# Rotary embedding on one core: the first store is issued right after its own row, and three one-element copies that held two stores are taken out

## The chip, the cores and the metric

The kernel runs on 1 core of a Trainium2 chip. A core has several engines that run side by side, each with its own instruction queue: VectorE (DVE in the profile), ScalarE (ACT), GpSimd (POOL), TensorE (PE, not used here) and SyncE (SP). They meet through semaphores. Data move between the memory of the chip (HBM) and the core's SBUF (128 partitions) by DMA: an engine issues a transfer, and 16 DMA engines carry it out.

The metric is the device time of one execution in microseconds (us), as the median of several runs. Before: 316.28 us, median of 3 runs (316.09 to 316.48). Less is better.

## The reference

`x` has 8 batches x 2048 positions x 16 heads x 64 numbers, all float32. Neighbouring pairs of the 64 are rotated by an angle that depends on the position:

```python
x_pairs = x.reshape(batch, seq_len, num_heads, head_dim // 2, 2)
x1 = x_pairs[..., 0]
x2 = x_pairs[..., 1]
out1 = x1 * cos - x2 * sin
out2 = x1 * sin + x2 * cos
out = np.stack([out1, out2], axis=-1).reshape(batch, seq_len, num_heads, head_dim)
```

`cos` and `sin` have 2048 x 32 numbers. Input and output are 67.1 MB each, and the arithmetic is three operations per number.

## The kernel before

**Tiling.** One batch is called a row here. The 2048 positions of a row are laid over 128 partitions, 16 positions (K) to each, so that a row is a tile of 128 partitions x 16,384 numbers. Rows are kept in bf16 in `xt`, a buffer with five places; `HOME` says which row has which place: rows 0 to 4 have a place each, and rows 5, 6 and 7 take over those of rows 0, 1 and 2. In HBM a row is float32, 8.39 MB; in SBUF it is bf16, half of that, and the conversion is done by the DMA itself.

**Work on a row.** `rotate(b)` makes three VectorE operations: L89 writes `qt` = row x sine table, L92 multiplies the row in its place by the cosine table, L97 adds `qt`, with the two of each pair swapped, to the row. `qt` is one buffer (the pool has one slot), so that each rotation reuses it. Row 0 is rotated in two pieces, 4 positions and 12.

**Order.** The order is written out by hand (`manual_schedule`); each engine works through its instructions in program order, and the semaphore waits follow from the tiles that an instruction reads and writes.

- SP loads the first 4 positions of row 0 as float32 (L101), ACT converts them (L108).
- POOL issues, one behind the other and all on one DMA queue (q0 in the profile): the rest of row 0 (L102), the cosines and sines (L103, L104), `load(1, 2)` for rows 1 and 2 in one transfer, `load(3, 2)` for rows 3 and 4 (L70 is the line inside `load`).
- VectorE makes the tables (L110 to L112) and rotates row 0.
- `rotate(1)`, then `rotate(2)` with `between=first_store`: after L89 of row 2, `first_store` puts two copies of one element on ACT. L120 copies the last element of `qt` into `gate`, so ACT waits for L89 of row 2. L121 copies an element of row 0 onto itself, so that it counts as a writer of row 0; `store(0, 1)` (L74 inside `store`), which reads row 0, waits for it.
- L126 copies one element of the last place of `xt` (row 4) into `mark` on POOL, so POOL waits there until `load(3, 2)` has landed. Then come, on POOL, `store(1, 2)` (waits for row 2's rotation), `load(5, 1)` (takes row 0's place, so it waits until `store(0, 1)` has landed) and `load(6, 2)` (waits for `store(1, 2)`).
- `rotate(3)`, `rotate(4)`, `store(3, 2)`, `rotate(5)`, `rotate(6)`, `store(5, 2)`, `rotate(7)`. The last row is converted to float32 by ACT in four pieces (L138) into places 3 and 4 of `xt` (`wide`) and stored by SP (L139) on a queue of its own (q1).

Of the kernel before, what the change touches and what calls it, by code (L numbers as in the profile page):

```python
# [2 lines left out]

# [4 lines left out]


@with_exitstack  # L10
def kernel(
    ctx: ExitStack,
    tc: tile.TileContext,
    x: bass.AP,
    cos: bass.AP,
    sin: bass.AP,
    out: bass.AP,
):
    nc = tc.nc
    fp32 = mybir.dt.float32  # L20
    bf16 = mybir.dt.bfloat16
    mult = mybir.AluOpType.mult
    add = mybir.AluOpType.add

    B, S, H, D = x.shape
    P = 128
    K = S // P
    KP = 16
    D2 = D // 2
    HD = H * D  # L30
    NX = 5
    HEAD = 4
    PART = 4
    STAGE = 3


    HOME = [0, 1, 2, 3, 4, 0, 1, 2]

    x_t = x.rearrange("b (p k) h d -> b p k (h d)", p=P, k=K)
    out_t = out.rearrange("b (p k) h d -> b p k (h d)", p=P, k=K)  # L40
    x_r = x.rearrange("b (p k) h d -> p b (k h d)", p=P, k=K)
    out_r = out.rearrange("b (p k) h d -> p b (k h d)", p=P, k=K)
    cos_t = cos.rearrange("(p k) c -> p (k c)", p=P, k=K)
    sin_t = sin.rearrange("(p k) c -> p (k c)", p=P, k=K)

    consts = ctx.enter_context(tc.tile_pool(name="consts", bufs=1))
    stage = ctx.enter_context(tc.tile_pool(name="stage", bufs=1))

    xt = consts.tile([P, NX, K * HD], bf16)
    cos_sb = consts.tile([P, K * D2], fp32)  # L50
    sin_sb = consts.tile([P, K * D2], fp32)
    c_tab = consts.tile([P, K, D], bf16)
    s_tab = consts.tile([P, K, D], bf16)

    wide = (
        xt[:, STAGE : STAGE + 2]
        .rearrange("p a c -> p (a c)")
        .bitcast(fp32)
        .rearrange("p (k c) -> p k c", c=HD)
    )  # L60

    gate = consts.tile([1, 1], bf16)
    mark = consts.tile([1, 1], bf16)

    def home(b, k0=0, k1=K):
        return xt[:, HOME[b], k0 * HD : k1 * HD].rearrange("p (k c) -> p k c", c=HD)

    def load(b, n):
        h = HOME[b]
        nc.gpsimd.dma_start(out=xt[:, h : h + n], in_=x_r[:, b : b + n])  # L70

    def store(b, n):
        h = HOME[b]
        nc.gpsimd.dma_start(out=out_r[:, b : b + n], in_=xt[:, h : h + n])  # L74

    def rotate(b, k0=0, k1=K, between=None):
        nk = k1 - k0
        xp = home(b, k0, k1)
        qt = stage.tile([P, KP, HD], bf16, name="qt", tag="work")

        def rows(a):
            return a.rearrange("p k (h e) -> p k h e", h=H, e=D)

        def tab(a):
            return dataclasses.replace(
                a, offset=a.offset + k0 * D, ap=[a.ap[0], [D, nk], [0, H], [1, D]]
            )

        nc.vector.tensor_tensor(out=rows(qt[:, :nk]), in0=rows(xp), in1=tab(s_tab), op=mult)  # L89
        if between is not None:  # L90
            between(qt)
        nc.vector.tensor_tensor(out=rows(xp), in0=rows(xp), in1=tab(c_tab), op=mult)  # L92
        q_swap = dataclasses.replace(
            qt, offset=qt.offset + 1, ap=[qt.ap[0], [2, nk * HD // 2], [-1, 2]]
        )
        x3 = xp.rearrange("p k (a j) -> p (k a) j", j=2)
        nc.vector.tensor_tensor(out=x3, in0=x3, in1=q_swap, op=add)  # L97

    with tc.manual_schedule():
        head = stage.tile([P, HEAD, HD], fp32, name="st", tag="work")  # L100
        nc.sync.dma_start(out=head[:, :HEAD], in_=x_t[0, :, :HEAD])  # L101
        nc.gpsimd.dma_start(out=home(0, HEAD), in_=x_t[0, :, HEAD:])  # L102
        nc.gpsimd.dma_start(out=cos_sb, in_=cos_t)  # L103
        nc.gpsimd.dma_start(out=sin_sb, in_=sin_t)  # L104
        load(1, 2)
        load(3, 2)

        nc.scalar.copy(out=home(0, 0, HEAD), in_=head[:, :HEAD])  # L108
        s2 = s_tab.rearrange("p k (i j) -> p (k i) j", j=2)
        nc.vector.tensor_copy(out=s2[:, :, 0], in_=sin_sb)  # L110
        nc.vector.tensor_scalar_mul(s2[:, :, 1], sin_sb, -1.0)  # L111
        nc.vector.tensor_copy(  # L112
            out=c_tab.rearrange("p k (i j) -> p (k i) j", j=2),
            in_=cos_sb.to_broadcast([P, K * D2, 2]),
        )
        rotate(0, 0, HEAD)
        rotate(0, HEAD, K)

        def first_store(qt):
            nc.scalar.copy(out=gate, in_=qt[:1, KP - 1, HD - 1 :])  # L120
            nc.scalar.copy(out=xt[:1, HOME[0], :1], in_=xt[:1, HOME[0], :1])  # L121
            store(0, 1)

        rotate(1)
        rotate(2, between=first_store)
        nc.gpsimd.tensor_copy(out=mark, in_=xt[:1, 4, K * HD - 1 :])  # L126
        store(1, 2)
        load(5, 1)
        load(6, 2)
        rotate(3)  # L130
        rotate(4)
        store(3, 2)
        for b in range(5, B):
            rotate(b)
            if b == 6:
                store(5, 2)
        for k in range(0, K, PART):
            nc.scalar.copy(out=wide[:, k : k + PART], in_=home(B - 1, k, k + PART))  # L138
        nc.sync.dma_start(out=out_t[B - 1], in_=wide)  # L139


# [1 line left out]
_INS = ['x', 'cos', 'sin']  # L143
_OUTS = [((8, 2048, 16, 64), 'float32')]


# [23 lines left out]
```

## Time and profile before

The profiled execution has a span of 314.3 us from the first to the last instruction; what lies around the span is in the run's time and not in the profile.

| what | value |
|---|---|
| median of 3 runs | 316.28 us |
| lowest and highest | 316.09, 316.48 us |
| span of the profiled execution | 314.3 us |
| granted clock | 1.000 |
| L89, L92, L97 each, on a whole row | 8.69 us, 7 times |
| VectorE waits for loads (L89) | 34.3 us in 3 waits, the longest 12.4 us |
| POOL waits: for L121 / for L97 / for stores to land (L70) | 93.4 / 91.5 / 43.1 us |
| last row's conversion on ACT (L138) | 4 x 3.60 us, from 269.31 |
| last store, issue to landing | 30.0 us, issued at 283.46 |

The transfers on q0 in the order of issue, with the time of issue and the time from there to landing (us):

| transfer | issued | to landing |
|---|---|---|
| rest of row 0 | 1.25 | 21.1 |
| rows 1 and 2 in | 3.0 | 59.3 |
| rows 3 and 4 in | 3.7 | 97.3 |
| row 0 out (first store) | 97.91 | 22.5 |
| rows 1 and 2 out (second store) | 115.04 | 44.1 |
| row 5 in | 120.67 | 57.6 |
| rows 6 and 7 in | 159.44 | 57.4 |
| rows 3 and 4 out | 167.52 | 88.0 |
| rows 5 and 6 out | 243.40 | 55.6 |

How to read it: "busy" is the time in which an engine executes; an instruction that waits for a semaphore is idle time in front of it, and the profile names what ended it ("releaser"). In lines of the timeline, the first number is the start in us from the span's start, the second the duration in us, and the bracket the idle time before and its releaser. A POOL line of the kind DMA_DIRECT2D is the issue of a transfer, not the transfer. The row "DMA" of the page gives the busy share of the 16 DMA engines in 40 slices of the span in tenths (9 is 90% or more); in a stretch, a share near 1 means that all 16 had work throughout, and it can come out a little over 1, since packets are long against the stretch and a packet on its border is counted on one side. The GB/s count the SBUF side of a transfer, which for loads is half the size of the HBM side.

### The profile page before, as it was taken

How to read it: one execution, taken by the hardware profiler on the slowest of the kernel's cores; microseconds unless marked ns; L12 is line 12 of the kernel's file. 1: busy time of each engine (PE TensorE's matmuls, PEld its weight loads, DVE VectorE, ACT ScalarE, POOL GpSimd, SP SyncE). 2: the span in 40 equal slices, each digit the busy share in tenths (PEclk: the TensorE clock that was granted, in tenths of full speed). 3: DMA queues.
4: the chain of work that ended last, by engine and by line, in shares of the span. 5: the costliest groups of instructions: out<-in, count | busy, mean ns of one | idle time of the engine just before them, and what ended most of it. 6: DMA issues, size and time to landing. Idle time of an engine off the chain costs nothing.

```text
span 314.3 us, 114 instructions
## 1 busy us (share of the span) xinstructions
DVE 210.3 (67%) x30; ACT 19.3 (6%) x8; POOL 12.4 (4%) x16
## 2 busy tenths in 40 slices
DVE  0009995099999999999992299903999999200000
ACT  1030000000000000000000000000000000790000
POOL 4000000000002400000000000000000000000000
DMA  7999999999999999999999999999999999999996
GB/s 253 264 284 200 200 200 267 200 200 204 263 200 267 409 525 400 400 425 509 400 200 225 242 200 200 234 234 334 400 509 425 400 400 525 409 400 400 525 409 267
DMA packets 2512, 102.24 MB, mean 325 GB/s; under 512 B 208, under 2 KB 208, under 8 KB 336
## 3 DMA queue, kind: packets, MB, share of 16 engines
q0 software_dynamic: 2224, 91.75, 92.1%
q1 hardware_dynamic: 288, 10.49, 8.0%
HBM read 67.63 MB, written 67.11 MB: 429 GB/s over the span
## 4 chain that ended last, share of the span: by engine, by line
DVE 67%; another core or an unknown queue 11%; ACT 3%; ACTq 1%; issue 0%; DVEq 0%
DVE xt L92 22%; DVE xt L97 22%; DVE qt L89 22%; ACT xt L138 3%; ACTq L165 1%; DVE c_tab L112 0%; DVEq L89 0%; DVEq L92 0%
## 5 line engine op out<-in xcount | busy, mean ns | idle before, releaser
L89 DVE TENSOR_TENSOR qt<-xt,s_tab 128x16384 bf16<-128x16384 bf16 (+2 forms) x9 | 69.7, 7743 | 34.5 <-DMA xt<-in_x_dram 34.3
L92 DVE TENSOR_TENSOR xt<-xt,c_tab 128x16384 bf16<-128x16384 bf16 (+2 forms) x9 | 69.7, 7743 | 0.4
L97 DVE TENSOR_TENSOR xt<-xt,qt 128x16384 bf16<-128x16384 bf16 (+2 forms) x9 | 69.7, 7743 | 0.3
L138 ACT CAST xt<-xt 128x4096 f32<-128x4096 bf16 x4 | 14.1, 3601 | 171.7 <-DVE xt L97 171.7
L110 DVE CAST s_tab<-sin_sb 128x512 bf16<-128x512 f32 x1 | 0.5, 454 | 23.8 <-DMA sin_sb<-in_sin_dram 23.8
L74 POOL DMA_DIRECT2D out_dram<-xt x4 | 2.7, 670 | 184.9 <-ACT xt L121 93.4
L126 POOL COPY mark<-xt 1x1 bf16<-1x1 bf16 x1 | 5.0, 5019 | 2.6 <-DMA xt<-in_x_dram 2.6
L120 ACT COPY gate<-qt 1x1 bf16<-1x1 bf16 x1 | 0.2, 192 | 78.6 <-DVE qt L89 78.6
L70 POOL DMA_DIRECT2D xt<-in_x_dram x4 | 2.7, 696 | 43.1 <-DMA out_dram<-xt 43.1
L108 ACT CAST xt<-st 128x4096 bf16<-128x4096 f32 x1 | 3.6, 3605 | 13.1 <-DMA st<-in_x_dram 13.1
L108 ACT ACT_TABLE_LOAD x1 | 1.3, 1283 | 0.7 <-PEq L154 0.7
L102 POOL DMA_DIRECT2D xt<-in_x_dram x1 | 0.7, 680 | 0.8 <-PEq L165 0.8
L112 DVE CAST c_tab<-cos_sb 128x1024 bf16<-128x1024 f32 x1 | 0.7, 685 | 0.0
L103 POOL DMA_DIRECT2D cos_sb<-in_cos_dram x1 | 0.6, 569 | 0.0
L104 POOL DMA_DIRECT2D sin_sb<-in_sin_dram x1 | 0.6, 562 | 0.0
L111 DVE TENSOR_SCALAR s_tab<-sin_sb 128x512 bf16<-128x512 f32 x1 | 0.4, 444 | 0.0
L121 ACT COPY xt<-xt 1x1 bf16<-1x1 bf16 x1 | 0.2, 188 | 0.0
L154 POOL MEMSET const-float32-0.0<- 128x1 f32 x1 | 0.1, 99 | 0.2 <-issue 0.2
L154 POOL MEMSET const-bfloat16-1.0<- 128x1 bf16 x1 | 0.1, 102 | 0.0
L154 POOL MEMSET const-float32-1.0<- 128x1 f32 x1 | 0.1, 99 | 0.0
L154 POOL MEMSET const-uint8-127<- 128x1 uint8 x1 | 0.1, 99 | 0.0
## 6 DMA issues: line engine op xcount, KB each, us to landing
xt<-in_x_dram POOLq DMA_DIRECT2D x3, 8192.0 KB, 59.3
xt<-in_x_dram POOLq DMA_DIRECT2D x1, 4096.0 KB, 57.6
xt<-in_x_dram POOLq DMA_DIRECT2D x1, 3072.0 KB, 21.1
st<-in_x_dram SPq DMA_DIRECT2D x1, 2048.0 KB, 14.4
cos_sb<-in_cos_dram POOLq DMA_DIRECT2D x1, 256.0 KB, 21.2
sin_sb<-in_sin_dram POOLq DMA_DIRECT2D x1, 256.0 KB, 21.3
out_dram<-xt POOLq DMA_DIRECT2D x4, 49.9
out_dram<-xt SPq DMA_DIRECT2D x1, 30.0
```

The lines of the kernel that those rows point to most:

```text
L70: nc.gpsimd.dma_start(out=xt[:, h : h + n], in_=x_r[:, b : b + n])
L74: nc.gpsimd.dma_start(out=out_r[:, b : b + n], in_=xt[:, h : h + n])
L89: nc.vector.tensor_tensor(out=rows(qt[:, :nk]), in0=rows(xp), in1=tab(s_tab), op=mult)
L92: nc.vector.tensor_tensor(out=rows(xp), in0=rows(xp), in1=tab(c_tab), op=mult)
L97: nc.vector.tensor_tensor(out=x3, in0=x3, in1=q_swap, op=add)
L102: nc.gpsimd.dma_start(out=home(0, HEAD), in_=x_t[0, :, HEAD:])
L103: nc.gpsimd.dma_start(out=cos_sb, in_=cos_t)
L108: nc.scalar.copy(out=home(0, 0, HEAD), in_=head[:, :HEAD])
L112: nc.vector.tensor_copy(out=c_tab.rearrange("p k (i j) -> p (k i) j", j=2), in_=cos_sb.to_broadcast([P, K * D2, 2]),)
L126: nc.gpsimd.tensor_copy(out=mark, in_=xt[:1, 4, K * HD - 1 :])
L138: nc.scalar.copy(out=wide[:, k : k + PART], in_=home(B - 1, k, k + PART))
L165: with _tile.TileContext(nc) as tc:
```

## The change

`store(0, 1)` moves up in the program to stand right behind the rotation of row 0, where it waits for that rotation alone. The copies L120, L121 and L126 go, with the tiles `gate` and `mark`, and `rotate` loses the parameter that let `first_store` run in its middle. `store(1, 2)` stays where it was; ahead of it on POOL there is now only the first store. All transfers keep their sizes and their order on POOL.

```diff
-    gate = consts.tile([1, 1], bf16)
-    mark = consts.tile([1, 1], bf16)
-
...
-    def rotate(b, k0=0, k1=K, between=None):
+    def rotate(b, k0=0, k1=K):
...
-        if between is not None:
-            between(qt)
...
         rotate(0, 0, HEAD)
         rotate(0, HEAD, K)
 
-        def first_store(qt):
-            nc.scalar.copy(out=gate, in_=qt[:1, KP - 1, HD - 1 :])
-            nc.scalar.copy(out=xt[:1, HOME[0], :1], in_=xt[:1, HOME[0], :1])
-            store(0, 1)
-
+        store(0, 1)
         rotate(1)
-        rotate(2, between=first_store)
-        nc.gpsimd.tensor_copy(out=mark, in_=xt[:1, 4, K * HD - 1 :])
+        rotate(2)
         store(1, 2)
         load(5, 1)
         load(6, 2)
```

## The prediction

> **What bounds the kernel now.** I read the page first: the span, the share of each engine, the DMA rows.
>
> ```profile
> span 314.3 us, 114 instructions
> DVE 210.3 (67%) x30; ACT 19.3 (6%) x8; POOL 12.4 (4%) x16
> ...
> DMA  7999999999999999999999999999999999999996
> ...
> q0 software_dynamic: 2224, 91.75, 92.1%
> q1 hardware_dynamic: 288, 10.49, 8.0%
> HBM read 67.63 MB, written 67.11 MB: 429 GB/s over the span
> ```
>
> No compute engine is near full (DVE 67%), but the DMA row is at 9 in all slices but the first and the last: the kernel is a stream of 134.7 MB at 429 GB/s. The chain of waits puts 67% on DVE and 11% on "another core or an unknown queue"; it follows DVE because the last store hangs on the last rotation, but the three pieces of 10.57, 11.05 and 12.33 us without an owner are DVE waiting for loads. So I ask when the 16 DMA engines lack work, and cut the span at the landings (issue time plus the time from issue to landing of that transfer). Columns: stretch, its length, DVE, ACT and POOL busy, clock, DMA share, GB/s.
>
> ```profile
> 62.00:101.00 39.00, 38.44 (x5) 0.29 (x2) 0.55 (x1) 1.00 1.00 229
> 101.00:120.60 19.60, 19.48 (x3) 0.00 (x0) 5.72 (x2) 1.00 1.00 428
> 120.60:159.40 38.80, 38.56 (x6) 0.00 (x0) 0.57 (x1) 1.00 1.01 419
> 159.40:178.30 18.90, 7.82 (x1) 0.00 (x0) 1.42 (x2) 1.00 1.03 222
> 178.30:216.90 38.60, 26.07 (x3) 0.00 (x0) 0.00 (x0) 1.00 1.01 231
> 216.90:255.50 38.60, 38.41 (x5) 0.00 (x0) 0.70 (x1) 1.00 1.02 435
> ```
>
> Each stretch holds one transfer: rows 3 and 4 in, row 0 out, rows 1 and 2 out, row 5 in, rows 6 and 7 in, rows 3 and 4 out. The share is 1.00 or more in all six. Loads show half the GB/s because the bf16 side is counted; by the HBM side (8.39 MB a row) rows 6 and 7 are 16.78 MB in 38.6 us, 435 GB/s, and rows 3 and 4 out the same. Thus the end moves only if the DMA engines get a gap or lose one.
>
> The third view is the order in time around the change.
>
> ```profile
> 97.32 0.19 ACT L120 COPY gate<-qt 1x1 bf16<-1x1 bf16 x1 [78.56 <-DVE qt L89]
> 97.33 8.69 DVE L92 TENSOR_TENSOR xt<-xt,c_tab 128x16384 bf16<-128x16384 bf16 x1
> 97.42 0.19 ACT L121 COPY xt<-xt 1x1 bf16<-1x1 bf16 x1
> 97.91 0.55 POOL L74 DMA_DIRECT2D out_dram<-xt  x1 [93.43 <-ACT xt L121]
> 101.04 5.02 POOL L126 COPY mark<-xt 1x1 bf16<-1x1 bf16 x1 [2.58 <-DMA xt<-in_x_dram]
> ...
> 115.04 0.70 POOL L74 DMA_DIRECT2D out_dram<-xt  x1 [8.98 <-DVE xt L97]
> 120.67 0.57 POOL L70 DMA_DIRECT2D xt<-in_x_dram  x1 [4.92 <-DMA out_dram<-xt]
> ...
> 159.44 0.70 POOL L70 DMA_DIRECT2D xt<-in_x_dram  x1 [38.20 <-DMA out_dram<-xt]
> 167.52 0.72 POOL L74 DMA_DIRECT2D out_dram<-xt  x1 [7.37 <-DVE xt L97]
> ```
>
> Here the reader is to see that the first store (97.91) is already in the queue 3.1 us before the load ahead of it lands (101.04, where the mark's wait ends), and that the second (115.04) waits 8.98 us for DVE after the mark, not for the mark.
>
> **The change, part by part.**
>
> The first store's issue. Its row is rotated at 45.20 + 6.56 = 51.76 us. POOL has nothing in hand then (idle from 4.5 to 97.91 but for waits), so the issue goes from 97.91 to about 51.9, with its 0.55 us on POOL. On POOL it passes nothing: the five loads stand before it in program order and the second store behind it, in both kernels. In q0 it passes nothing either: the loads of rows 1 and 2 (landing 62.33, where DVE resumes) and of rows 3 and 4 (101.04) are both in the queue from 3.0 and 3.7 us, landing 59.3 and 97.3 us after issue, one after the other. So the transfer still follows rows 3 and 4, starts at about 101 and lands at 97.91 + 22.5 = 120.4. Gain in the queue: the gap between the old issue and the end of the load, which is none (share 1.00 in the stretches on both sides).
>
> What does a store cost the loads it waits behind? The same kernel shows it. The store of rows 3 and 4 is issued at 167.52 behind row 5 (landing 178.27) and rows 6 and 7 (216.86), and lands 88.0 us later, at 255.5. The load that ran with that store behind it took 216.86 - 178.27 = 38.6 us; the load of rows 3 and 4, alone until its last 3.1 us, took 101.04 - 62.33 = 38.7 us. The price lies between -0.1 and, if the noise of two landings goes the other way, +0.1 us; I take 0. The hand-over itself: row 0 out took 120.4 - 101.04 = 19.4 us, half of rows 3 and 4 out (38.6 / 2) is 19.3, and by POOL's wait it ends 0.3 us later, at 120.67: between 0 and 0.3 us could be won by a longer lead; I take 0, as the nearer row.
>
> The two ACT copies (L120, L121): 0.19 us each, 0.38 us in all. ACT idles 78.56 us before them and 171.7 us before L138. Nothing waits but the first store. 0.
>
> The mark (L126): 5.02 us on POOL, from 101.04 to 106.06, covered by the 8.98 us in which POOL then waits for DVE L97 (ends 114.74). Without it the second store still waits for that line: 115.04, 0. Were the cover gone, 5.0 us of POOL would delay the issue, and DMA would not feel it until the first store lands (120.4), 5.4 us after the present issue.
>
> Waits that go with the copies. `qt` of row 2 no longer has a reader on ACT, `xt` none on POOL. The chain spends 0.10 us between L89 and L92 of row 4 (149.71 to 149.81) where 0.02 is usual, so up to 0.08 us of DVE goes. It falls into the 11.17 us that DVE idles at 167.22 for row 5. 0. No wait is added: the one that the first store keeps, for row 0's rotation, ends at 51.76, before the old one.
>
> What is late next: the load of row 5 waits for the first store's landing, unchanged at 120.4; the second store is issued at 115.04 and the queue runs on.
>
> Sum: 0 + 0 + 0 + 0 = 0 us, between -0.4 (0.1 + 0.3) and +0.1. The span stays 314.3 us. The median of before is 316.28 us, 1.94 us more than this span of 314.34, which I leave as it is: **316.3 us**.
>
> **Rivals.**
>
> *Descriptors held by DVE (faster).* The store was issued under DVE L92 (97.33 to 106.02); the mark, which reads SBUF on POOL, took 5.02 us for one element and ended with L92. If the store's own descriptors had been held as long, the DMA engines would have stood still from 101.04 to 106.02, and the new issue, in DVE's idle time from 51.76 to 62.42, would win 5.0 us: 316.28 - 5.0 = 311.3. Against it: row 0's 8.39 MB went out between 101.04 and 120.4 at share 1.00, 433 GB/s, which leaves no room for 5 us. Chance 0.03.
> The Trainium skill, page "SBUF — State Buffer", section "SBUF: two separate sides", states that GpSimd is locked out of the port while VectorE runs in a two-port mode and cannot write a software DMA's descriptors; by that rule the sum would be about 311.3 us. The mark's 5.02 us agree with such a lock, the 1.00 of the next stretch does not agree that it reached the store.
>
> *Shared service (slower).* If the early store were served in turn with the load of rows 1 and 2, from 52.4 (51.9 + 0.55) on, that load's last 9.9 us (to 62.33) would take twice as long and land at 72.2. Rows 1 and 2 then end 9.9 us later, at 124.6, and the second store comes at 124.9 instead of 115.04; the queue, emptied of row 0 and rows 3 and 4 at 120.4 as before, would stand idle 124.9 - 120.4 = 4.5 us, and up to 3.1 us more for the pick-up (the first store was taken up within the 3.1 us from 97.91 to 101.04). The load of row 5 cannot fill the gap, as it stands behind the second store on POOL. 4.5 to 7.6 us, the lower nearer: 321 to 324, say 321.5. It decides once rows 1 and 2 land more than 5.4 us late (120.4 - 115.04). If the store went wholly ahead, its 19.4 us would make the gap 14 us: 330. For it: a store behind two loads this early in the kernel is not in the trace. Against it: every pair in q0 went in order, loads behind stores (row 5 behind rows 1 and 2) and a store behind two loads (rows 3 and 4). Chance 0.09, with any other loss over 0.2%.
> The Trainium skill, page "DMA: Bandwidth & Descriptors", section "Queues, rings and completion order", has each DMA engine take turns between queue rows, packet by packet, but keep order within one; by turns the time would be the 321.5. The trace lists all the software transfers under q0, so the rule would bite only if the store went to another queue.
>
> *It does not happen.* If POOL could not place the store until the load of rows 1 and 2 landed (62.33), the store would be queued later than said but still 39 us ahead of its turn: 316.3, no difference in time. The issue may slip to 97.91, where it is now, at no cost. Chance 0.04, inside "same".
>
> *Gain at the hand-over.* The bound above, -0.4 us: 315.9, inside 0.2% as well. Only a chain of such gains at later borders would pass it. Chance 0.02 beyond.
>
> **How the numbers follow.** 0.2% of 316.28 is 0.63 us, about what a measurement of this kernel can tell from no change (its three runs spread 0.39 us). Forecast with the hand-over's small gain: 0.82; store not placed early: 0.04; shared service or another loss: 0.09; descriptors: 0.03; a gain beyond the bound: 0.02. Within 0.2%: 0.86; slower 0.09; faster 0.05. The likeliest case spans 315.9 to 316.6 (the bounds, and the runs' spread of 0.2 up). I widen to the measurement's limit, 315.7 to 316.9; the other cases, 0.14 together, stay outside.
>
> **What would show it.** Right: the first store issued near 52 us and landing near 120.4, some 68 us from issue; the loads landing at 62.3 and 101.0; the second store at 115.0; DMA share 1.00 from 101 to 120.6; the last store issued near 283.4. Wrong: DVE's wait before row 1 longer than 10.7 us, or the second store after 120 with a gap in the DMA row (shared service); row 0 landing near 115.5 (descriptors); any load over 38.9 us for two rows (a store behind it is not free).

## The result, and the profile after

The changed kernel takes 317.15 us (median of 9 runs, 316.99 to 317.34), the kernel before 316.42 us in the same comparison (9 runs, 316.06 to 317.00). The ratio is 1.0028, 95% interval 1.0019 to 1.0036: slower by 0.2 to 0.4%. The forecast was no difference, 316.3 us with a range of 315.7 to 316.9; 317.15 lies above it. Two of these nine runs of the kernel before are at 317; in the comparisons below its medians are 316.15 to 316.27 us, and most versions with the early store are about 1.0 us above them.

The lines of the changed kernel's page that answer to those of before:

```profile
span 315.4 us, 110 instructions
DVE 210.4 (67%) x30; ACT 19.0 (6%) x6; POOL 7.4 (2%) x15
...
DMA  7999999999999999999999999999999999999996
...
HBM read 67.63 MB, written 67.11 MB: 427 GB/s over the span
```

The bytes are the same and the DMA row looks the same, but 429 GB/s have become 427: the same stream has lost about 1 us somewhere (315.4 - 314.3). The timeline of the changed kernel says where (in its numbering L86, L87 and L92 are the three operations of a rotation, L71 is the store, L67 the load; columns: start, duration, instruction, idle time before and what ended it):

```profile
52.35 0.56 POOL L71 DMA_DIRECT2D out_dram<-xt  x1 [47.87 <-DVE xt L92]
62.39 8.69 DVE L86 TENSOR_TENSOR qt<-xt,s_tab 128x16384 bf16<-128x16384 bf16 x1 [10.63 <-DMA xt<-in_x_dram]
...
115.01 0.71 POOL L71 DMA_DIRECT2D out_dram<-xt  x1 [62.10 <-DVE xt L92]
121.73 0.58 POOL L67 DMA_DIRECT2D xt<-in_x_dram  x1 [6.02 <-DMA out_dram<-xt]
...
160.35 0.70 POOL L67 DMA_DIRECT2D xt<-in_x_dram  x1 [38.04 <-DMA out_dram<-xt]
...
179.42 8.69 DVE L86 TENSOR_TENSOR qt<-xt,s_tab 128x16384 bf16<-128x16384 bf16 x1 [12.35 <-DMA xt<-in_x_dram]
```

The first store is issued at 52.35 in place of 97.91, row 1 starts at 62.39 as before (62.42), the second store is issued at 115.01 as before (115.04). Then row 5's load comes at 121.73 where it came at 120.67: the first store has landed 1.06 us later. From there all stays late by 0.9 to 1.1 us: the next load 160.35 (159.44), DVE's row 5 179.42 (178.39), the last store 284.52 (283.46). So the microsecond is lost between 62.4 and 121.7, on the DMA engines.

The DMA view of the stretch from 92 to 108 us, first before, then after, narrows it. It has 40 slices of 0.4 us, and a packet is counted in the slice where it begins, so a group of digits stands for 16 packets, one on each engine, that begin together.

```profile
DMA  0099000099000079000039000039000039000039
```

```profile
DMA  0099000099000099000000099000099000099000
```

Before, the groups follow each other at 6 slices, 2.4 us, throughout; the fourth group is the first of row 0's store. After, one step has 9 slices, 3.6 us: between the last packets of rows 3 and 4 in and the first of row 0 out. The packet records themselves say that these last 16 packets of the load took 3.25 to 3.81 us (mean 3.55) in place of 2.43 to 2.45; every other packet of a whole row, before and after this border, takes 2.42 to 2.50. The border costs 3.55 - 2.45 = 1.10 us, and the span is 1.04 us longer. The GB/s of two stretches show the same from another side (columns as in the prediction's table of stretches):

```profile
62.00:101.00 39.00, 38.47 (x5) 0.00 (x0) 0.00 (x0) 1.00 0.96 202
101.00:120.60 19.60, 19.53 (x3) 0.00 (x0) 0.71 (x1) 1.00 1.00 428
```

The stretch up to 101 moved 229 GB/s before and 202 now: 27 GB/s over 39 us is 1.05 MB, just the 16 packets of 65,536 B that used to begin before 101. (The packet records give 32,768 B to a packet of a row's load and 65,536 B to one of a row's store, so the GB/s count the side that is written. That this is the SBUF side, as said under "Time and profile before", holds for loads only.)

### The profile page after: what moved, and what is told of

It reads as the page before. It is cut to its first block, busy times and chain, and to the rows that moved or that the text cites. A ratio compares the mean times of both kernels' runs of the same rounds, so it can differ in the third digit from the quotient of the medians.

```text
span 315.4 us, 110 instructions
## 1 busy us (share of the span) xinstructions
DVE 210.4 (67%) x30; ACT 19.0 (6%) x6; POOL 7.4 (2%) x15
## 4 chain that ended last, share of the span: by engine, by line
DVE 67%; another core or an unknown queue 11%; ACT 3%; ACTq 1%; issue 0%; DVEq 0%
DVE xt L87 22%; DVE xt L92 22%; DVE qt L86 22%; ACT xt L128 3%; ACTq L155 1%; DVE c_tab L107 0%; DVEq L86 0%
## 5 line engine op out<-in xcount | busy, mean ns | idle before, releaser
L86 DVE TENSOR_TENSOR qt<-xt,s_tab 128x16384 bf16<-128x16384 bf16 (+2 forms) x9 | 69.7, 7743 | 35.6 <-DMA xt<-in_x_dram 35.4
L87 DVE TENSOR_TENSOR xt<-xt,c_tab 128x16384 bf16<-128x16384 bf16 (+2 forms) x9 | 69.7, 7744 | 0.3
L92 DVE TENSOR_TENSOR xt<-xt,qt 128x16384 bf16<-128x16384 bf16 (+2 forms) x9 | 69.7, 7744 | 0.3
L71 POOL DMA_DIRECT2D out_dram<-xt x4 | 2.7, 672 | 192.7 <-DVE xt L92 192.7
L67 POOL DMA_DIRECT2D xt<-in_x_dram x4 | 2.7, 697 | 44.1 <-DMA out_dram<-xt 44.1
## 6 DMA issues: line engine op xcount, KB each, us to landing
cos_sb<-in_cos_dram POOLq DMA_DIRECT2D x1, 256.0 KB, 21.2
sin_sb<-in_sin_dram POOLq DMA_DIRECT2D x1, 256.0 KB, 21.3
```

## The experiments

All times are medians beside runs of the kernel before on the same chip; the ratio stands with its 95% interval. "The border" is the one between the load ahead of the first store and that store; its step is the mean distance from the begin of the load's last 16 packets to the begin of the store's first 16, from the packet records (2.45 us before, 3.55 after).

### Which of the three edits

**e1: the store moved, the mark kept.** The rest as in the changed kernel.

```diff
         rotate(2)
+        nc.gpsimd.tensor_copy(out=mark, in_=xt[:1, 4, K * HD - 1 :])
         store(1, 2)
```

> The first store moved up as in the change, the mark (L126) kept. Lead theory (a first store that has long stood in the queue costs about 1.0 us at the border between rows 3 and 4 in and row 0 out): 317.1 us, and the load of row 5 is issued near 121.7 as in the changed kernel, not at 120.67. Mark theory (what is lost comes from the absence of the mark, or of POOL being held by it): 316.3 us, row 5 at 120.7.

317.15 us, ratio 1.0029 (1.0018 to 1.0040); border 3.37; row 5 issued at 121.62. The mark also serves as a clock, since it waits for rows 3 and 4 to land:

```profile
101.98 4.08 POOL L119 COPY mark<-xt 1x1 bf16<-1x1 bf16 x1 [49.06 <-DMA xt<-in_x_dram]
```

They land at 101.98 where they landed at 101.04: the load is late, not only the store behind it.

**e2: the gate kept, the mark gone.**

```diff
         rotate(2, between=first_store)
-        nc.gpsimd.tensor_copy(out=mark, in_=xt[:1, 4, K * HD - 1 :])
         store(1, 2)
```

> The gate kept (first store near 97.9), the mark taken out. Lead theory: 316.3 us as before, row 5 issued near 120.7. Mark theory: 317.1 us, row 5 near 121.7.

316.15 us, ratio 0.9998 (0.9988 to 1.0007); border 2.47, with one packet of 16 at 2.80. The mark costs nothing and saves nothing. What counts is when the first store is issued.

### How much lead it takes

**e3, e4 and e8: the first store held until 71.8, 89.3 and 93.6 us.** No mark in any of them; e3 runs `first_store` inside row 1's rotation, e4 behind it with the gate on row 1's result, e8 adds seven copies on ACT to e4's wait. The diff is e8's; e4 is without the loop.

```diff
+        def first_store():
+            nc.scalar.copy(out=gate, in_=xt[:1, HOME[1], K * HD - 1 :])
+            for _ in range(7):
+                nc.scalar.copy(out=cos_sb, in_=cos_sb)
+            nc.scalar.copy(out=xt[:1, HOME[0], :1], in_=xt[:1, HOME[0], :1])
+            store(0, 1)
...
         rotate(1)
+        first_store()
         rotate(2)
```

> No mark; the first store is released after the first operation of row 1 (near 71.7) in place of row 2 (97.9), so its lead over the border near 101 is 29 us, with the load of rows 1 and 2 already landed. Lead theory in its strong form (any long lead costs): 317.1 us, row 5 near 121.7. Theory that the loss comes from issuing the store while rows 1 and 2 are still arriving (before 62.3): 316.3 us, row 5 near 120.7.

> No mark; the first store is released after the last operation of row 1 (near 89.1), a lead of 12 us, five packets of 2.41 us. If the loss sets in with the store's descriptors being there before the last packets of the load, 317.1 us and row 5 near 121.7; if it grows with the lead or needs more than this, between 316.3 and 317.1; if it needs the earlier issue, 316.3 and row 5 near 120.7.

> No mark; the first store is released near 93.5 to 95 (seven copies of 128x512 on ACT behind row 1's last operation), a lead of 6 to 7.5 us, two or three packets. Issued at 89.3 it cost 1.0 us, at 97.9 nothing. If the loss needs the store's descriptors to be there before the end of the load's descriptors is fetched, the boundary lies somewhere between: 317.2 us if before this point, 316.2 if after it.

e3: 317.19 us, 1.0030 (1.0019 to 1.0041), border 3.58. e4: 317.18 us, 1.0030 (1.0020 to 1.0040), border 3.24. e8: 317.22 us, 1.0031 (1.0020 to 1.0043), border 3.46; its DMA view from 92 to 108 us has the same long step:

```profile
DMA  0099000099000099000000099000099000099000
```

The price does not grow with the lead: leads of 49, 29, 12 and 7.4 us (to the 101.04 of before; 7.4 is e8) all pay about 1 us; the 3.1 us of before (97.91) pay nothing. Between 93.6 and 97.9 lies the point where the price sets in, and no run narrows it further; the load's last packets begin between 97.9 and 98.2, and the late store's issue ends at 98.46, after they have begun. That rows 1 and 2 are still arriving at 52 us has nothing to do with it (e3).

### What the border needs

**e5: the store ahead of rows 3 and 4.** The changed kernel with the two transfers in the other order on q0.

```diff
         load(1, 2)
-        load(3, 2)
...
         store(0, 1)
+        load(3, 2)
         rotate(1)
```

> No gate and no mark; on POOL the load of rows 3 and 4 is moved behind the first store, so q0 holds rows 1 and 2 in, row 0 out, rows 3 and 4 in. Row 0 then lands near 82, rows 3 and 4 near 120.7. Three readings of the 1.0 us at the border of load and first store: (a) it belongs to the first store after loads that stands in the queue early: the last packets of rows 1 and 2 in (near 59 to 62) take 3.4 to 3.8 us in place of 2.43, and the time is 317.2; (b) it belongs to a place in the queue (so many transfers or descriptors since the start): no long packet at that border, and perhaps one elsewhere; (c) it needs a lead over a border of two rows that ends near 101, whatever follows: a long packet there or none, but not near 62. Time 316.2 with no long packet, 317.2 with one on all engines.

317.44 us, 1.0038 (1.0024 to 1.0052). The long step has moved with the store, as the DMA view from 53 to 69 us shows (same slices of 0.4 us):

```profile
DMA  0009900009900009900000009900009900009900
```

The border near 62 has a step of 3.74 us, and the last packets of rows 1 and 2 take up to 4.01 us; the border behind rows 3 and 4 in, near 120, has a step of 2.43. This is reading (a).

**e6: the tables on SP's queue; e7: rows 1 to 4 in four loads.** Two transfers fewer, or two more, ahead of the border on q0.

```diff
-        nc.gpsimd.dma_start(out=cos_sb, in_=cos_t)
-        nc.gpsimd.dma_start(out=sin_sb, in_=sin_t)
+        nc.sync.dma_start(out=cos_sb, in_=cos_t)
+        nc.sync.dma_start(out=sin_sb, in_=sin_t)
```

```diff
-        load(1, 2)
-        load(3, 2)
+        load(1, 1)
+        load(2, 1)
+        load(3, 1)
+        load(4, 1)
```

> The changed kernel with the cosines and sines loaded by SP on q1 in place of POOL on q0: two transfers fewer stand before the border on q0. If the 1.0 us comes at a fixed place in the queue, counted in descriptors or transfers, the long packets (over 3 us) move to a later border or into the middle of a transfer, or go; if it belongs to this load and this store, the last packets of rows 3 and 4 in stay at 3.4 to 3.8 us and the time near 317.2.

> The changed kernel with rows 1 to 4 loaded by four transfers of one row in place of two of two rows: two transfers more before the border, and the load ahead of the first store has the store's shape. If the 1.0 us comes from the change of shape from two rows to one, or from a place in the queue, it goes or moves; if it belongs to the first early store after loads, the last packets of row 4 in take 3.4 to 3.8 us and the row's store lands 1.0 us late. Rows 1 and 3 come in 19 us earlier, which lets the second store be issued earlier, but not row 0's.

e7: 317.23 us, 1.0033 (1.0020 to 1.0046), border 3.30. Neither the shape of the load nor, by e5 and e7, a place in the queue matters. e6 is far from 317.2: 333.69 us, 1.0552 (1.0536 to 1.0568): the tables land so late that DVE starts at 55.6 and the DMA engines run dry from 121.1 to 137.5. Its border still has a step of 2.97 us, with a store issued at 84.19; it says little more.

**e15: a later store of one row; e14: a first store of two rows.** e15 is the kernel before with rows 3 and 4 stored one by one, the first of them issued 56 us ahead of its turn. e14 has no gate and no mark and stores rows 0 and 1 together.

```diff
         rotate(3)
+        store(3, 1)
         rotate(4)
-        store(3, 2)
+        store(4, 1)
```

```diff
-        store(0, 1)
         rotate(1)
+        store(0, 2)
         rotate(2)
-        store(1, 2)
+        store(2, 1)
```

> The kernel before (late first store, mark kept), but rows 3 and 4 are stored by two transfers of one row; the one of row 3 is issued right behind the load of rows 6 and 7, some 57 us before its turn near 217. Shape theory: long packets at that border near 217 and 317.2 us. First-store theory: none, 316.2 us. Lead theory without any exception: 317.2 as well.

> No gate and no mark; the first store is of rows 0 and 1 together, issued after row 1's rotation near 89 with a lead of 12 us over the border near 101 (e4: one row with that lead lost 1.0 us), and row 2 is stored alone after its rotation. Shape theory (a store of one row, waiting behind a load, loses): no long packets near 101, row 2's load successor unaffected, 316.2 us. First-store theory: long packets near 101, 317.2 us.

e15: 316.12 us, 0.9996 (0.9986 to 1.0006); no packet over 2.55 us at either border. e14: 317.15 us, 1.0026 (1.0015 to 1.0037), border 3.40. So it is not the shape of the store either: the first store pays, at one row or two, and a later one does not, even when it is queued 56 us ahead. That is also what the changed kernel shows at its second such border, rows 3 and 4 out behind rows 6 and 7 in, where the store had waited 50 us (the DMA view from 209 to 225 us):

```profile
DMA  0099000099000099000099000099000099000099
```

All steps have 6 slices.

### What pays for it

**e9, e10, e11 and e13: a small store beforehand.** The changed kernel with 64 KB more to write, ahead of the first row's store: on SP's queue near 15 us (e9), on q0 ahead of everything (e10), on q0 behind the tables (e11), and on q0 ahead of everything but to row 0's own place (e13). What it writes is written over later. e12 adds e10's store to the kernel before.

```diff
+        nc.sync.dma_start(out=out_t[B - 1, :, 0, :128], in_=head[:, 0, :128])
```

```diff
+    small = consts.tile([P, 128], bf16)
...
+        nc.gpsimd.memset(small, 0.0)
+        nc.gpsimd.dma_start(out=out_t[B - 1, :, 0, :128], in_=small)
         nc.gpsimd.dma_start(out=home(0, HEAD), in_=x_t[0, :, HEAD:])
```

> The changed kernel with one small store added, early and on SP's queue q1: 512 B of each partition (64 KB) of the float32 head of row 0 go to row 7's place in the output near 15 us, where the last store overwrites them. First-write theory (the first write from the DMA engines to the output costs about 1.0 us and blocks what stands ahead of it, and it is paid once per kernel): the packets at the border near 101 go back to 2.4 to 2.5 us, row 5 is issued near 120.7 plus the small store's cost (under 0.5 us), time 316.2 to 316.7. Theory that it is the first store of its queue q0 that pays: long packets stay (over 3 us) near 101, time 317.2 or more.

> The changed kernel with a small store (64 KB, zeros, to row 7's place, overwritten later) issued by POOL on q0 ahead of everything else, when the queue is empty. If the first store of q0, or of the kernel, pays once, it pays here, where nothing stands ahead of it: no long packets near 101; the loads start later by the memset, the issue and the small transfer (0.5 to 2.5 us, of which part lies beside the head's load on q1), time 316.2 to 317.5 with the border clean. If each first load-to-store border pays, whatever went before: long packets stay, time 317.2 plus the delay.

> The same small store on q0, but behind the loads of row 0's rest and the tables, ahead of rows 1 and 2: it stands in the queue some 18 us before its turn, near 23 us. If the first store behind loads pays once: a stretch of about 1 us without large packets or with long ones appears near 22 to 24, and the border near 101 is clean: 317.2 us, the cost moved and not removed. If the payment belongs to a full-size store of a row: long packets near 101 stay, 317.3 or more.

> The kernel before (late first store, mark kept) with the small store on q0 ahead of everything else. It has no long packets to lose, so it shows the small store's own price at the start: 316.2 plus 0 to 1.5 us. If e10 comes out equal to this run, the early issue costs nothing once the first store has been paid for; if e10 is 1.0 us above it, the small store did not pay.

> As e10 (changed kernel, small store on q0 ahead of everything else), but the small store goes to row 0's own place, 512 B of each partition's 64 KB. If the 1.0 us is paid for the first write to that part of the output, the packets near 101 go back to 2.45 us and the time to 316.4, that of e12. If it belongs to the shape of the store, or to the first large store, they stay over 2.9 us and the time at 317.2.

| run | median, us | ratio (95%) | border, us |
|---|---|---|---|
| e9 | 317.31 | 1.0039 (1.0024 to 1.0054) | 3.05 |
| e10 | 317.22 | 1.0036 (1.0023 to 1.0048) | 3.21 |
| e11 | 317.17 | 1.0032 (1.0019 to 1.0045) | 3.23 |
| e13 | 317.13 | 1.0031 (1.0021 to 1.0042) | 3.18 |
| e12 | 316.42 | 1.0006 (0.9997 to 1.0015) | 2.46 |

None takes the price away; e10 is 0.8 us above e12, which has the same small store. All four borders are shorter than 3.55 (by 0.3 to 0.5 us), but e4 without any small store is at 3.24, so nothing can be made of that. That the part of the output is written for the first time is not the cause (e13).

**e18: the small store waits early, the row's store comes late.** The kernel before, with the first 128 numbers of each partition of row 0 stored by an instruction right behind its rotation. These numbers belong to the first of row 0's two pieces, so the store is issued at 32.72, not near 52, and waits 68 us for its turn.

```diff
         rotate(0, HEAD, K)
+        nc.gpsimd.dma_start(out=out_t[0, :, 0, :128], in_=xt[:, 0, :128])
```

> The kernel before (row 0's store late, near 97.9), with a store of 64 KB of row 0 (its first 128 numbers of each partition) issued on q0 right after row 0's rotation, near 52 us, so that it waits behind rows 3 and 4 in. If a store of any size that waits there sets the load's last packets back: they take over 2.9 us, 317.2 us and a little. If it needs the row's store itself (its size or its packets of 64 KB): no long packets, 316.2 to 316.6.

318.75 us, 1.0082 (1.0067 to 1.0097): neither number. But the load's last packets take 2.43 to 2.45 us, so a waiting store of 64 KB does not set them back. The time went elsewhere: L122, the copy of an element of row 0 onto itself, now has to wait for the small store to land, and the row's store comes too late.

```profile
101.35 0.19 ACT L122 COPY xt<-xt 1x1 bf16<-1x1 bf16 x1 [3.74 <-DMA out_dram<-xt]
101.86 0.55 POOL L74 DMA_DIRECT2D out_dram<-xt  x1 [68.59 <-ACT xt L122]
```

The border is 4.94 us wide, 2.49 more than 2.45, which is the 2.5 us lost. It also shows the price of issuing into an empty queue: from the issue at 101.86 to the first packet at 102.97 are 1.1 us.

**e16 and e17: a store of 2.1 MB beforehand.** The changed kernel also stores the float32 head of row 0 to row 7's place, on SP's queue (e16) or on q0 between the tables and rows 1 and 2 (e17).

```diff
+        nc.sync.dma_start(out=out_t[B - 1, :, :HEAD], in_=head[:, :HEAD])
```

```diff
+        nc.gpsimd.dma_start(out=out_t[B - 1, :, :HEAD], in_=head[:, :HEAD])
         load(1, 2)
         load(3, 2)
```

> The changed kernel with 2.1 MB more to write: SP stores the float32 head of row 0 to row 7's place on q1 near 15 us (overwritten by the last store). At 434 GB/s it costs 4.8 us of DMA. If any store of some size pays once for the core: the border near 106 has no long packets, time 316.2 + 4.8 = 321.0. If q0 pays for itself, or a store this size doesn't pay: long packets there, 322.0.

> The same 2.1 MB stored by POOL on q0, behind the rest of row 0 and the tables and ahead of rows 1 and 2, issued near 15 us with a lead of some 8 us over its turn near 23. If the first sizeable store of q0 that waits behind loads pays once: the border near 106 has no long packets, and a stretch of about 1 us may be lost near 23 instead; 321.0 to 322.0. If the payment belongs to the first store behind a run of large load packets: long packets near 106, 322.0.

e16: 322.03 us, 1.0186 (1.0170 to 1.0201). By the time that is the number of the second theory; the packets say the first. The border, now near 106, is clean (DMA view from 98 to 114 us):

```profile
DMA  0099000099000099000099000099000099000099
```

Its step is 2.43 us, no packet over 2.43. The last packets of rows 3 and 4 begin at 103.95 instead of 98.02, 5.9 us later, of which the added store explains 4.8 by its bytes: 1.1 us went earlier, before the border. The packet records place most of it around the added store, which is issued at 15.37 and has its first packets at 20.30: the last three packets of row 0 on each engine take 1.90, 2.12 and 2.48 us on average in place of 1.83, 1.0 us in all. e17: 322.78 us, 1.0204 (1.0187 to 1.0221); border 2.67, 0.2 us too long, nine of 16 packets over 2.6. Here the earlier loss lies between row 0's last packets and the next large ones, those of the added store (the tables lie between): 4.29 us, against 3.08 before to the packets of rows 1 and 2, 1.2 us more. At the border one packet took 3.22 us, and one engine stays behind to the end: the last packet of the kernel ends 0.93 us after the mean of its 16, against 0.18 before, and the span is 321.4 us where e16 has 320.3. So an earlier store of 2.1 MB takes the price over, wholly on the other queue, for most engines on the same one. It moves the loss; it does not save it.

### What this leaves

Shown: the price is about 1.0 us, once in an execution; the first sizeable store pays it when it stands in the loads' queue 7.4 us or more before its turn behind large packets; it lies in the last packets of the load ahead, on all 16 engines; when that store is issued as those packets begin, it is not paid. Not shown: what the DMA engines do in it, why a late issue escapes it, and how large a store or its packets must be (64 KB does not pay, 2.1 MB does; each has 128 packets, as a row has, but of 512 B and 16 KB in place of 64 KB). Of the 87 runs of the kernel before, 79 lie between 316.04 and 316.53 us and 8 between 316.82 and 317.16; no run with the early store is under 316.99. One engine that pays is enough to lengthen an execution (in e2's profile, with its single packet of 2.80, the span is 314.6 us instead of 314.3), but none of the 8 has a trace, so whether they paid is not shown. No version beat the kernel before: e2, which only drops the mark, and e15 equal it.

## Why the prediction was wrong

*What bounds the kernel* was right, and it is why so small a cause can be seen at all: the DMA engines have no slack, so 1.10 us at one border became 1.04 us of span, with DVE and POOL waiting for it.

*The step that failed* is "What does a store cost the loads it waits behind?". It put the price between -0.1 and +0.1 us, from the row where the store of rows 3 and 4 waits 49 us behind a load. The row was read rightly, and the changed kernel repeats it (the clean view from 209 to 225 us). But it is not a row of the same thing: that store is the third of the kernel, and the moved one is the first. The load that it was compared with, that of rows 3 and 4, does end at the first store, but had it behind it for 3.1 us only, a lead that does not pay. For the first store the price is about 1.0 us (e1, e3, e4, e5, e8, e14). The bound "between 0 and 0.3 us could be won" at the hand-over brought nothing: from the landing of rows 3 and 4 to that of row 0 it is 19.4 us in both kernels. The prediction did say, under the shared service, that "a store behind two loads this early in the kernel is not in the trace"; this should have widened the sum's bounds, not only fed a chance of 0.09.

*The first store's issue*: on POOL and in q0 it passes nothing, as said. Its issue at 52.35 (51.9 predicted), the order on q0 and the second store at 115.01 (115.0) came as written; the landing came 1.06 us late by row 5's issue.

*The two ACT copies and the mark at nothing*: right for the mark by e2 (0.9998), and for the copies by e3, which has them with an early store and takes 317.19 us, where the changed kernel without them takes 317.15. That the mark was covered by the 8.98 us of waiting for DVE is seen in e1, where it ends at 106.06 and the second store still comes at 115.05. The DVE time of the dropped waits, up to 0.08 us, was there: from the first to the second operation of row 4 it was 8.80 us (141.01 to 149.81) and is 8.72 (140.93 to 149.65). DVE then waits for row 5, as said.

*The rivals.* Descriptors held by DVE: no gain appeared, and e18's store, issued at 101.86 in the middle of a DVE operation that runs to 106.10, had its first packets at 102.97, while the mark behind it ended with that operation (102.40 + 3.74 = 106.14). That the operation runs in the two-port mode which the rule named there needs is not shown by any run. Shared service: the sign was right and the mechanism wrong; row 1's wait is 10.63 us (10.66) and the second store is on time, so the load of rows 1 and 2 was not disturbed. That the store would not be placed early did not come about: it was issued at 52.35. Gain at the hand-over: there was none.

*The signs to look for* included "any load over 38.9 us for two rows (a store behind it is not free)". That is the one that came true: in the changed kernel the load of rows 3 and 4 lands 98.3 us after its issue in place of 97.3, 39.7 us after rows 1 and 2, and e1's mark shows the same, 0.94 us later.

## What to carry to other kernels

In a kernel bound by DMA, an early issue is not free just because the queue keeps its order: look at the packets on both sides of the border. To price a wait by a row of the same trace, the row has to be alike in whatever may matter, its being the first of its kind among them. A delay that looks idle, such as the gate, may be well placed: taking out one of several such delays at a time (e1, e2) showed in two runs which one counted.

## What the runs showed of the hardware

- The first sizeable store, waiting in the queue behind large loads, lengthens the load's last packets from 2.43 us to 3.2 to 3.7 us (means of the 16 engines: e1, e3 to e5, e7, e8, e14 and the changed kernel), once; later stores that wait 50 and 56 us do not.
- A store issued into a drained queue needs 1.1 us to its first packet (e18).
- Small transfers on a second queue suffer beside large packets. In e6 the two tables, 256 KB each, went by q1. DVE's longest wait for them, in the list of waits of e6 (total, times, longest):

```profile
DVE s_tab L105 <- DMA sin_sb<-in_sin_dram: 55.6, 1, 55.6
```

From issue to landing they took 32.0 and 54.0 us, where on q0 it was 21.2 and 21.3 (the list of DMA issues of e6, last column):

```profile
cos_sb<-in_cos_dram SPq DMA_DIRECT2D x1, 256.0 KB, 32.0
sin_sb<-in_sin_dram SPq DMA_DIRECT2D x1, 256.0 KB, 54.0
```

On q1 they follow the head, which lands near 15 us; the second table is there near 55, 40 us later. Each engine has 8 + 8 small packets to pass, and one of them after each large packet of 2.43 us makes 39 us. The Trainium skill, page "DMA: Bandwidth & Descriptors", section "Queues, rings and completion order", says that a DMA engine takes turns between the queue rows that have work, packet by packet. The run agrees, with one small packet of 2,048 B to a turn: from 35 us on the 16 engines' table packets begin 2.5 us apart, one behind each large packet.
